# Pinning the TensorE instructions of the expert rounds to the order in which the kernel emits them

## The chip, the cores and the metric

The kernel runs on one core of one Trainium2 chip. The core has TensorE (PE in the profile, its weight loads PEld), VectorE (DVE), ScalarE (ACT), GpSimd (POOL) and the queue of SyncE (SP), which issues most of the transfers from HBM. The metric is the device time of one execution in microseconds (us), the median of several runs.

## The reference

Two blocks of two layers each work on 256 tokens of 1024 features in float32. Each of the four layers has a token mixer (RWKV-7, dilated attention, and twice a mixture of differential and sparse attention), and behind it a layer of 32 experts. The change lies in the expert layer alone. A router picks for each token one of four groups and two of its eight experts. The reference runs every expert over all tokens and multiplies by the gates, which are zero for experts that were not picked:

```python
hid = silu(einsum('td,edf->tef', xt, w_gate[gi])) * einsum('td,edf->tef', xt, w_up[gi])
hid = hid * gates[:, gi, :, None]
out = out + einsum('tef,efd->td', hid, w_down[gi])
```

The expert weights are the bulk of the input: per layer 32 experts with three matrices of 1024 x 256 numbers.

## The kernel before

The kernel is recorded through a tile layer whose scheduler decides the order of instructions on each engine. It ranks what is ready by a time model of its own, so TensorE's instructions may stand in another order than the Python code emits them. `keep_in_program_order` binds one instruction behind the one that was emitted before it on the same engine. It adds no wait for a semaphore, only a place in the queue.

An expert layer ("stage" below; there are four in a run, stage 1 to 4) gathers the tokens of each expert into 64 slots and works in 16 rounds, `g` = 0 to 15, two experts to a round. The rounds are written in `rounds_of`, and one round emits these parts for TensorE, in this order:

- `gate_up(g)` (line 331): 32 matmuls with 64 output rows, for the gate and the up matrix. The profile counts two records to each, since the operands are float32, so a round shows 64. ScalarE's Silu (line 334) and VectorE's product (line 336) make `hid` of the two results.
- `scatter(g - 1)` (line 366): 8 matmuls of 128 x 512 that add the last round's output rows `yh` and `yl` to the four accumulators `psc` (two token tiles by two halves of the features).
- `hid_t(g)` (line 342): two transposes of `hid`, which VectorE copies to `hT` (line 344).
- `scat(g + 1)` (lines 313 and 317): 6 small matmuls that make the scatter matrix and the gates of the next round.
- `gather`, two parts (line 300): 16 matmuls that collect the tokens of the next pair of rounds. In rounds 14 and 15 there is none.
- `down(g)` (line 353): 8 matmuls with 64 output rows, 16 records. VectorE (line 356, in stages 1 and 2 only) and the split of line 117 and 118 make `yh` and `yl` of them.

Matmuls with 64 output rows carry the form 128*64 in the profile, the others 128*128. Weights come in tiles of 1 MiB from 14 buffers, six tiles to a round, and round `g` asks for those of round `g + 3`; SyncE issues a load when the tile that held the buffer before has been read. Before round 0 stand `scat(0)` and all of `gather(0)`; behind round 15 comes the last `scatter`, and then a branch that skips further rounds when no expert has more than 64 tokens. They are skipped here: VectorE's line 336 ran 64 times in the whole execution, 16 rounds in each of four stages.

Of the kernel before, what the change touches and what calls it, by code (L numbers as in the profile page):

```python
# [26 lines left out]
P = 128  # L27
# [3 lines left out]
KD = 8  # L31
# [5 lines left out]
class Net:  # L37
# [17 lines left out]
    def wtile(self, name, own=False):  # L55
        """the next of the weight buffers, in turn with the extra ones where they are open"""
        pool, tag = self.wp, "w"
        if len(self.slots) > self.nw and not own:
            self.turn = (self.turn + 1) % len(self.slots)
            pool, tag = self.slots[self.turn]  # L60
        return pool.tile([P, 2048], F32, tag=tag, name=self.nm(name))
# [20 lines left out]
    def open_extra(self, n):  # L82
        """n more weight buffers, on the right side"""
        pool = self.extra.enter_context(self.tc.tile_pool(name=self.nm("extra"), bufs=n, side="right", reuse_waits="tile"))
        if len(self.slots) == self.nw:
            self.turn = -1
        self.slots += [(pool, "e")] * n
# [5 lines left out]
    def consts(self, scratch):  # L93
        nc = self.nc
        c = self.const
        jp = scratch        # [p, f] = f - p
# [5 lines left out]
        self.tri = c.tile([P, P], F32R, name="tri")         # [i, t] = 1 where t >= i  # L102
# [3 lines left out]
        self.iota64 = c.tile([P, CAP], F32, name="iota64")   # 1, ..., 64  # L106
# [8 lines left out]
    def split(self, hi, lo, src, eng=None):  # L115
        """hi + lo = src, each a float32r value."""
# [3 lines left out]
    def transpose_fm(self, dst, src):  # L120
        """dst[p, k, tok] = src[tok, tt, k, p]"""
# [17 lines left out]
class Moe:  # L139
    """w_g, w_u [32, 1024, 256]; w_d [32, 256, 1024]; scale [128, 512] x 2 multiplies the result"""  # L140
# [33 lines left out]
    def take(self, tt, xp, parts=False):  # L174
        """xp: the tokens of the tile tt [tok, k, p], feature 8p + k; parts: leaves their float32r parts in fs [p, k, t]"""
# [31 lines left out]
    def route(self):  # L207
# [16 lines left out]
        # the first of the largest  # L224
        v.tensor_tensor_scan(cu.rearrange("p t g -> p (t g)"), N.first4.rearrange("p t g -> p (t g)"),
                             t4.rearrange("p t g -> p (t g)"), 0.0, op0=OP.mult, op1=OP.add)
        # the two largest of each group, the first where they are equal
# [12 lines left out]
        # place of a token among those of its expert, from 1; 0 elsewhere  # L240
# [19 lines left out]
        # further rounds, for experts with more tokens than slots  # L260
# [18 lines left out]
    def rounds_of(self, load, acc, first, fills=None):  # L279
# [4 lines left out]
        w_g, w_u, w_d = self.w  # L284
        wt, xg, hid, hT, pt, gs, ys = {}, {}, {}, {}, {}, {}, {}
# [6 lines left out]
        def gather(b, k2):  # L292
# [3 lines left out]
            for kk in range(2):  # L296
                i = 0
                for tt in range(NT):
                    for xs in (xh, xl):
                        nc.tensor.matmul(ps[:, kk * 256:kk * 256 + 256], xs[:, tt, 2 * k2 + kk, :], pm[b][:, tt],  # L300
# [8 lines left out]
        def scat(g):  # L309
            b, o = g // 2, (g % 2) * P  # L310
            ps = N.psum("b")
            for tt in range(NT):
                nc.tensor.matmul(ps[:, tt * P:(tt + 1) * P], pm[b][:, tt, o:o + P], N.identr, start=True, stop=True)
            i = 0
            for tt in range(NT):
                for gp in (self.gh, self.gl):
                    nc.tensor.matmul(ps[:, 256:288], pm[b][:, tt, o:o + P], gp[:, tt], start=i == 0, stop=i == 3)  # L317
# [7 lines left out]
        def gate_up(g):  # L325
            b, o = g // 2, (g % 2) * P
            pg_, pu = N.psum("b"), N.psum("b")
            for nm, ps in (("g", pg_), ("u", pu)):
                for k in range(KD):
                    for c in range(2):  # L330
                        nc.tensor.matmul(ps[c * 64:c * 64 + 64, :256], xg[b][:, k, o + c * 64:o + c * 64 + 64],  # L331
# [7 lines left out]
        def hid_t(g):  # L339
            ps = N.psum("b")  # L340
            for j in range(2):
                nc.tensor.transpose(ps[:, j * P:(j + 1) * P], hid[g][:, j, :], N.ident)
# [3 lines left out]
        def down(g):  # L346
            yh = m2.tile([P, 2, 512], F32R, tag="yh", name=N.nm("yh"))
            yl = m2.tile([P, 2, 512], F32R, tag="yl", name=N.nm("yl"))
            for n in range(2):
                ps = N.psum("b")  # L350
                for j in range(2):
                    for c in range(2):
                        nc.tensor.matmul(ps[c * 64:c * 64 + 64, :], hT[g][:, j, c * 64:c * 64 + 64],  # L353
# [6 lines left out]
        def scatter(g):  # L360
# [4 lines left out]
            for i, tt, n in order:  # L365
                nc.tensor.matmul(acc[tt, n], pt[g][:, tt * P:(tt + 1) * P], ys[g][i][:, n], start=first and g == 0 and i == 0,
# [30 lines left out]
    def run(self, x, after_loads=None):  # L397
        """-> x + the sums of the experts, by token tile and half [128, 512], in PSUM"""
# [25 lines left out]
def rwkv_consts():  # L424
# [5 lines left out]
    for s in (16, 32):                                   # [t, i]: second block of two against the first  # L430
# [18 lines left out]
def wsplit(N, sp, w, eng=None, keep=False):  # L449
    """w [128, a, b] -> float32r parts, hi + lo = w; sp = pool, buffers of hi, of lo, and their tags"""  # L450
# [24 lines left out]
def weave(main, *fill, rest=True):  # L475
    """main's steps, with a step of the fillers (one after the other) behind each; then the rest of these"""
# [12 lines left out]
def every(gen, n):  # L489
    """a step of gen at each n-th of its own steps"""  # L490
# [9 lines left out]
def proj_fm_steps(N, sp, xh, xl, w, n0, evac, lay="(p k) n -> p k n"):  # L500
    """columns n0 .. n0+512 of x @ w, feature-major: evac(j, psum [128, 2 x 256]) for the tiles j, j + 1."""
# [3 lines left out]
    for k2 in range(KD // 2):  # L505
        wh, wl = wsplit(N, sp, parts[k2 // 2][:, 2 * (k2 % 2):2 * (k2 % 2) + 2])
        for lo in range(2):
            for j in range(4):
                o = pss[j // 2][:, (j % 2) * 256:(j % 2 + 1) * 256]
                ws = slice(j * P, (j + 1) * P)  # L510
                for kk in range(2):
# [4 lines left out]
                    else:  # L516
                        # the first product of a bank clears all of it
# [11 lines left out]
def proj_steps(N, sp, xh, xl, w, n0, evac, lay="(p k) n -> p k n", nk=KD):  # L529
    """columns n0 .. n0+512 of x @ w, token-major: evac(tt, psum [128, 512]).  The last step by token tile."""  # L530
# [22 lines left out]
def proj_tt(N, sp, xh, xl, w, n0, evac, lay="(p k) n -> p k n", subs="vggg", keep=True):  # L553
    """proj_steps by token tile, with all of the weights' parts on chip (sp may be one for each quarter): a step to split them,
    then one per token tile"""
# [15 lines left out]
def last_proj(N, sp, xh, xl, w, emit):  # L571
    """x @ w by halves, the second by token tile: emit(tt, n, psum [128, 512])"""
# [5 lines left out]
def split_tokens(N, xh, xl, tok, tt, eng=None):  # L578
    """tok(k): features k of the token tile tt [tok, 128] -> feature-major float32r parts"""
# [18 lines left out]
def rwkv(N, src, I, cst, emit, side, tail, scratch):  # L598
    """src: setup(tile) with tile() for [128, 8, 128], norm(tt), then tok(tt, k) gives [tok, p] (feature 8p + k); token
    mixing; emit(tt, n, psum [128, 512]).  Yields once before the last steps of the output projection."""  # L600
# [34 lines left out]
    pv = rp.tile([P, 7, KD], F32, name="pv")       # natural feature tiles: w0, a0 (by direction), k_k, k_a, r_k  # L635
# [20 lines left out]
    # ---- projections  # L656
# [16 lines left out]
    def shift(j, first=False):  # L673
        """the tokens mixed by mu[j], by halves of the features"""
# [72 lines left out]
    # ---- recurrence, in chunks of 64 tokens; the second direction runs on reversed tokens  # L747
# [5 lines left out]
    kn = p2.tile([P, KD, T], F32, name="kn")        # the removal key, normalised and negated  # L753
# [24 lines left out]
    def prep(z, e2, q2):  # L778
# [18 lines left out]
        E = q2.tile([P, 8, 65], F32, tag="E", name=N.nm("E"))           # 1, then the decay so far  # L797
# [81 lines left out]
    # inverses of the 16x16 diagonal blocks of I - N, a pair of chunks to a partition  # L879
# [40 lines left out]
    MQB = [p4.tile([P, 4, 4, P], F32, name=f"MQB{i}") for i in range(NB)]     # N, M, Q', B by pair  # L920
# [18 lines left out]
    def norm(z, e2):  # L939
        """group norm, bonus and output gate of 256 features: y in AR[z][e2][:, 0], (e, tt, 128) of each token"""  # L940
# [43 lines left out]
    def job(z, et, buf):  # L984
# [35 lines left out]
        # towards the chunk's end, and token-major  # L1020
# [52 lines left out]
        # inside the chunks  # L1073
# [7 lines left out]
        # [k, t] and [k', k] for the state's share; [v, t] and [v, k] of the chunk itself  # L1081
# [11 lines left out]
        RA = jp.tile([P, 2, 2, 2, 64], F32, tag="RA", name=N.nm("RA"), bufs=3)       # tile, (t | k), chunk  # L1093
# [49 lines left out]
    # ---- both directions, output projection  # L1143
# [45 lines left out]
def attn_consts():  # L1189
# [7 lines left out]
    a = np.stack(out, 1)                                        # [t, g, s]  # L1197
# [3 lines left out]
def dilated(N, src, I, cst, emit, tail=None):  # L1201
    """src: setup(tile) with tile() for [128, 1024], norm(tt), then tok(tt, k) gives [tok, p] (feature 8p + k);
    mixture of dilated attentions; emit(tt, n, psum [128, 512]).  Yields once before the output projection."""
# [114 lines left out]
def rope_setup(N, pos, c, scratch):  # L1318
    """cos | sin tables by token tile: cc [tok, tt, 2, 8] = cos, cos; ss = -sin, sin."""
# [32 lines left out]
def causal_setup(N, c):  # L1352
    """[t, 128 + s] = 0 where s <= t of a token tile, else -1e30; 0 before"""
# [8 lines left out]
def mixers(N, src, I, li, cs, caus, emit, tail=None):  # L1362
    """src: setup(tile), norm(tt), then tok(tt, k) gives [tok, p] (feature 128k + p); emit(tt, n, psum [128, 512]).
    Yields once before the output projection."""
# [15 lines left out]
    def fm_split(src, nk, tag, scale=1.0, ap=ap):  # L1380
        """src(tt, k) [128 tok, 128 features] -> feature-major float32r parts"""
# [660 lines left out]
```

## Time and profile before

| | |
|---|---|
| median of 3 runs | 2570.92 us (2564.14 to 2574.7) |
| span of the profiled execution | 2570.2 us |
| TensorE busy in it | 2341.1 us (91%) |
| mean granted clock of TensorE | 0.950 of full speed |

The span runs from the first to the last instruction of one execution. Its row is the nearest thing to that execution's own time that the profile has, and it stands 0.7 us below the median of the runs. A busy TensorE is not TensorE at its peak, since its matmuls overlap and their ends are modelled; where the text needs the length of something, it takes it from one start to another. Granted clock 1.00 is 2.4 GHz, the higher of the engine's two levels.

### The profile page before, as it was taken

Reading aid. Unit: us, or ns where it says so; the run is one execution under the profiler, and the core shown is the slowest. Engines: PE = TensorE matmul, PEld = TensorE weight load, DVE = VectorE, ACT = ScalarE, POOL = GpSimd, SP = SyncE. Lnnn points to the kernel's source line nnn. Section 1 sums busy time; section 2 is a strip of 40 time slices with the busy share of each in tenths; the row PEclk is TensorE's granted clock in tenths of the full one; section 3 lists DMA queues with packets and bytes.
Section 4 is the critical chain, followed back from the end, with each engine's and each line's share of the span. In section 5 each row is a group of like instructions: output and inputs, shape, how many; then the busy total and the mean of one; then the engine's idle time right before and its main releaser. Section 6 shows DMA issues by size and latency. Waiting matters only on the chain. (4 is left out here: it accounts for less than half of the span.)

```text
span 2570.2 us, 38418 instructions
## 1 busy us (share of the span) xinstructions
PE 2341.1 (91%) x15568; PEld 1682.7 (65%) x15568; DVE 1232.8 (48%) x2648; ACT 748.5 (29%) x1341; POOL 368.3 (14%) x292
## 2 busy tenths in 40 slices
PE   5976899988999799998999899989999799989997
PEld 2853577766665598986665477766665577766654
DVE  5678566764332435355332366573222576642222
ACT  2422243332111344442111235432111245421110
POOL 1243112230000221211000111220000222210000
PEclk7986899999999999998999889989999899989999
DMA  8425432258998362538999443477996443769993
GB/s 256 151 98 178 163 110 67 91 203 326 412 404 335 116 200 92 184 88 334 405 399 355 158 143 128 151 282 314 408 400 272 156 138 124 245 232 399 412 383 116
DMA packets 162988, 605.94 MB, mean 236 GB/s; under 512 B 36960, under 2 KB 37984, under 8 KB 107488
## 3 DMA queue, kind: packets, MB, share of 16 engines
q1 hardware_dynamic: 159072, 599.64, 62.4%
q0 software_dynamic: 3136, 3.16, 0.5%
q8 instruction: 131, 2.15, 0.3%
q10 hardware_dynamic: 576, 0.39, 0.1%
q14 instruction: 73, 0.60, 0.1%
HBM read 602.09 MB, written 1.05 MB: 235 GB/s over the span
## 5 line engine op out<-in xcount | busy, mean ns | idle before, releaser
L331 PE MATMUL psb<-w,xg 128*64 128x256 f32 x4096 | 474.3, 380 | 0.0
L331 PEld LDWEIGHTS psb<-w,xg 128*64 128x64 f32 x4096 | 297.8, 137 | 185.6 <-issue 48.1
L455 ACT ACTIVATE wh<-w 128x1024 fp32r<-128x1024 f32 x230 | 240.3, 1059 | 287.1 <-PE psb L545 147.7
L459 DVE TENSOR_TENSOR wl<-w,wh 128x1024 fp32r<-128x1024 f32 x150 | 202.6, 1357 | 167.8 <-ACT wh L455 142.5
L459 POOL TENSOR_TENSOR wl<-w,wh 128x1024 fp32r<-128x1024 f32 x80 | 198.3, 2481 | 576.6 <-ACT wh L455 466.4
L336 DVE SCALAR_TENSOR_TENSOR hid<-psb,gs,sg 128x256 f32<-128x256 f32 x64 | 43.0, 672 | 422.3 <-PE psb L331 422.3
L353 PE MATMUL psb<-w,hT 128*64 128x512 f32 x1024 | 234.1, 599 | 1.5 <-DVE hT L344 1.5
L544 PE MATMUL psb<-wh,xh 128*128 128x512 f32 x448 | 185.4, 415 | 5.6 <-ACT wh L455 2.4
L545 PE MATMUL psb<-wh,xl 128*128 128x512 f32 x448 | 181.3, 405 | 0.3 <-DVE xl L118 0.3
L118 DVE TENSOR_TENSOR yl<-psb,yh 128x512 fp32r<-128x512 f32 x128 | 88.4, 691 | 133.4 <-ACT yh L117 133.3
L117 ACT ACTIVATE yh<-psb 128x512 fp32r<-128x512 f32 x128 | 76.4, 597 | 255.9 <-DVE psb L356 140.7
L353 PEld LDWEIGHTS psb<-w,hT 128*64 128x64 f32 x1024 | 69.7, 136 | 118.3 <-issue 108.1
L542 PE MATMUL psb<-wl,xh 128*128 128x512 f32 x448 | 130.2, 398 | 3.3 <-POOL wl L459 1.7
L300 PE MATMUL psb<-pm,xh 128*128 128x256 f32 x512 | 130.7, 295 | 0.0
L321 ACT ACTIVATE pt<-psb 128x256 fp32r<-128x256 f32 x64 | 24.6, 384 | 347.9 <-PE psb L317 347.9
L300 PE MATMUL psb<-pm,xl 128*128 128x256 f32 x512 | 124.9, 283 | 0.0
L1742 PE MATMUL psb<-w,c_fm 128*32 128x512 f32 x384 | 85.6, 744 | 34.8 <-DMA w<-in_ada_w_dram 23.0
L544 PEld LDWEIGHTS psb<-wh,xh 128*128 128x128 f32 x448 | 86.5, 193 | 26.0 <-ACT wh L455 3.6
L542 PEld LDWEIGHTS psb<-wl,xh 128*128 128x128 f32 x448 | 84.9, 191 | 23.1 <-POOL wl L459 2.6
L545 PEld LDWEIGHTS psb<-wh,xl 128*128 128x128 f32 x448 | 86.9, 194 | 18.3 <-DVE xl L118 1.2
L300 PEld LDWEIGHTS psb<-pm,xl 128*128 128x128 f32 x512 | 98.7, 193 | 0.0
L300 PEld LDWEIGHTS psb<-pm,xh 128*128 128x128 f32 x512 | 98.6, 193 | 0.0
(540 smaller groups left out, 4167.3 us busy)
## 6 DMA issues: line engine op xcount, KB each, us to landing
w<-in_moe_w_gate_dram SPq DMA_DIRECT2D x64, 1024.0 KB, 7.8
w<-in_moe_w_up_dram SPq DMA_DIRECT2D x64, 1024.0 KB, 8.8
w<-in_moe_w_down_dram SPq DMA_DIRECT2D x64, 1024.0 KB, 10.0
w<-in_w_exp_gate_dram SPq DMA_DIRECT2D x64, 1024.0 KB, 7.9
w<-in_w_exp_up_dram SPq DMA_DIRECT2D x64, 1024.0 KB, 9.1
w<-in_w_exp_down_dram SPq DMA_DIRECT2D x64, 1024.0 KB, 10.4
w<-in_ada_w_dram SPq DMA_DIRECT2D x48, 1024.0 KB, 5.0
w<-in_w_in_dram SPq DMA_DIRECT2D x44, 1024.0 KB, 5.0
```

Of the source, the lines that this page charges most:

```text
L117: self.nc.scalar.activation(hi, src, AF.Copy)
L118: (eng or self.nc.vector).tensor_sub(lo, src, hi.bitcast(F32))
L300: nc.tensor.matmul(ps[:, kk * 256:kk * 256 + 256], xs[:, tt, 2 * k2 + kk, :], pm[b][:, tt], start=i == 0, stop=i == 3)
L331: nc.tensor.matmul(ps[c * 64:c * 64 + 64, :256], xg[b][:, k, o + c * 64:o + c * 64 + 64], wt[nm, 2 * g + c][:, k, :], start=k == 0, stop=k ...
L336: v.scalar_tensor_tensor(hid[g].rearrange("s j p -> s p j"), pu[:, :256].rearrange("s (p j) -> s p j", j=2), gs[g], sg.rearrange("s (p j) ...
L353: nc.tensor.matmul(ps[c * 64:c * 64 + 64, :], hT[g][:, j, c * 64:c * 64 + 64], wt["d", 2 * g + c][:, j, n * 512:(n + 1) * 512], start=j == ...
L455: nc.scalar.activation(wh, w, AF.Copy)
L459: i = (nc.gpsimd if eng == "g" else nc.vector).tensor_sub(wl, w, wh.bitcast(F32))
L542: nc.tensor.matmul(pss[tt], xh[:, k, t], wl[:, kk, :], start=False, stop=k == nk - 1)
L544: nc.tensor.matmul(pss[tt], xh[:, k, t], wh[:, kk, :], start=k == 0, stop=False)
L545: nc.tensor.matmul(pss[tt], xl[:, k, t], wh[:, kk, :], start=False, stop=False)
L1742: nc.tensor.matmul(ps[32 * j:32 * j + 32, :], self.c[:, k:k + 1].to_broadcast([P, 32]), wt[:, j * 512:(j + 1) * 512], start=k == 0, stop=k ...
```

## The change

Inside `rounds_of` every matmul goes through a helper `mm`, and each of the two transposes of `hid_t` likewise, and both call `keep_in_program_order`. Nothing else is altered but comments and docstrings. In the changed program the matmuls of these functions carry the line of the helper, 288, and lines below it are shifted by four.

```diff
+        keep = N.tc.keep_in_program_order
+
+        def mm(*a, **k):
+            keep(nc.tensor.matmul(*a, **k))
...
-                        nc.tensor.matmul(ps[:, kk * 256:kk * 256 + 256], xs[:, tt, 2 * k2 + kk, :], pm[b][:, tt],
+                        mm(ps[:, kk * 256:kk * 256 + 256], xs[:, tt, 2 * k2 + kk, :], pm[b][:, tt],
                                          start=i == 0, stop=i == 3)
...
-                nc.tensor.transpose(ps[:, j * P:(j + 1) * P], hid[g][:, j, :], N.ident)
+                keep(nc.tensor.transpose(ps[:, j * P:(j + 1) * P], hid[g][:, j, :], N.ident))
...
-                nc.tensor.matmul(acc[tt, n], pt[g][:, tt * P:(tt + 1) * P], ys[g][i][:, n], start=first and g == 0 and i == 0,
+                mm(acc[tt, n], pt[g][:, tt * P:(tt + 1) * P], ys[g][i][:, n], start=first and g == 0 and i == 0,
                                  stop=last and i == 1, skip_group_check=True)
```

What this moves on TensorE, outside the skipped further rounds, lies in three places. The first is round 10 of stage 1, where `psb_6402` and `psb_6403` are the gate and up results and `yh_6369`, `yl_6370` the output rows of round 9. Before, TensorE's queue read:

```order
L353 MATMUL psb_6379<-w_5937,hT_6335 64x512
L331 MATMUL psb_6402<-w_6044,xg_6235 64x256
L366 MATMUL psc_5148<-yh_6369,pt_6230 128x512
L366 MATMUL psc_5150<-yh_6369,pt_6230 128x512
L366 MATMUL psc_5148<-yl_6370,pt_6230 128x512
L366 MATMUL psc_5150<-yl_6370,pt_6230 128x512
L366 MATMUL psc_5149<-yh_6369,pt_6230 128x512
L366 MATMUL psc_5151<-yh_6369,pt_6230 128x512
L331 MATMUL psb_6402<-w_6046,xg_6235 64x256
```

and now, from the end of the same gate and up matmuls on, it reads:

```order
L288 MATMUL psb_6403<-w_6050,xg_6235 64x256
L288 MATMUL psc_5148<-yh_6369,pt_6230 128x512
L288 MATMUL psc_5149<-yh_6369,pt_6230 128x512
L288 MATMUL psc_5150<-yh_6369,pt_6230 128x512
L288 MATMUL psc_5151<-yh_6369,pt_6230 128x512
L288 MATMUL psc_5148<-yl_6370,pt_6230 128x512
L288 MATMUL psc_5149<-yl_6370,pt_6230 128x512
L288 MATMUL psc_5150<-yl_6370,pt_6230 128x512
L288 MATMUL psc_5151<-yl_6370,pt_6230 128x512
L346 MATMUL psb_6448<-ident,hid_6438 128x128 x2
```

The eight scatter matmuls had been put in between the gate and up matmuls; now they all stand behind them, ahead of the transposes of `hid`. This holds for rounds 9 to 15 of stages 1, 3 and 4 and rounds 8 to 15 of stage 2, 29 rounds. In stages 1 and 2 five or six of them had been split in three pieces as here (6 matmuls behind the first gate matmul, 2 behind the seventeenth), in stages 3 and 4 all eight stood behind the first gate matmul; the first split round of each stage had all eight behind the seventeenth, and round 15 began with two or five of them ahead of its first gate matmul. In some rounds 14 and 15 the eight matmuls of `down` had alternated between the two halves of the features; now the four of the first half come first. The rounds before the split ones are the same in both programs.

The second place is the start of stages 1 and 2, on TensorE behind the router's matmuls (`psb_5119`); `psb_5188` is `scat(0)`, `psb_5201` the first part of `gather(0)`. Before:

```order
L248 MATMUL psb_5119<-mask_5115,ones 128x32
L313 MATMUL psb_5188<-identr,pm_5130 128x128
L300 MATMUL psb_5201<-pm_5130,xh_4932 128x256
L313 MATMUL psb_5188<-identr,pm_5130 128x128
L300 MATMUL psb_5201<-pm_5130,xl_4933 128x256
L300 MATMUL psb_5201<-pm_5130,xh_4932 128x256
L300 MATMUL psb_5201<-pm_5130,xl_4933 128x256
L317 MATMUL psb_5188<-gh_5136,pm_5130 128x32
```

and now:

```order
L248 MATMUL psb_5119<-mask_5115,ones 128x32
L288 MATMUL psb_5188<-identr,pm_5130 128x128 x2
L288 MATMUL psb_5188<-gh_5136,pm_5130 128x32
L288 MATMUL psb_5188<-gl_5137,pm_5130 128x32
L288 MATMUL psb_5188<-gh_5136,pm_5130 128x32
L288 MATMUL psb_5188<-gl_5137,pm_5130 128x32
L288 MATMUL psb_5201<-pm_5130,xh_4932 128x256
```

Six gather matmuls that had stood among those of `scat(0)` now stand behind all of them. Stages 3 and 4 had this order already.

The third place is the last scatter of each stage, here on TensorE in stage 1, with `yh_6990` and `yl_6991` of round 15 and the four accumulators. Before:

```order
L366 MATMUL psc_5148<-yh_6990,pt_6893 128x512
L366 MATMUL psc_5150<-yh_6990,pt_6893 128x512
L366 MATMUL psc_5148<-yl_6991,pt_6893 128x512
L366 MATMUL psc_5150<-yl_6991,pt_6893 128x512
L366 MATMUL psc_5149<-yh_6990,pt_6893 128x512
L366 MATMUL psc_5151<-yh_6990,pt_6893 128x512
L366 MATMUL psc_5149<-yl_6991,pt_6893 128x512
L366 MATMUL psc_5151<-yl_6991,pt_6893 128x512
```

and now:

```order
L288 MATMUL psc_5148<-yh_6990,pt_6893 128x512
L288 MATMUL psc_5148<-yl_6991,pt_6893 128x512
L288 MATMUL psc_5149<-yh_6990,pt_6893 128x512
L288 MATMUL psc_5149<-yl_6991,pt_6893 128x512
L288 MATMUL psc_5150<-yh_6990,pt_6893 128x512
L288 MATMUL psc_5150<-yl_6991,pt_6893 128x512
L288 MATMUL psc_5151<-yh_6990,pt_6893 128x512
L288 MATMUL psc_5151<-yl_6991,pt_6893 128x512
```

The accumulators of the second half of the features (`psc_5149`, `psc_5151`) had come last; now the first token tile's two accumulators come first and those of the second tile last.

On the other engines little moves. In VectorE's queue the scaling of the second half (line 356) falls behind the split of the first half (line 118) in round 14 of stages 1 and 2 and round 15 of stage 2. In SyncE's queue one weight load of the following layer moves from behind the branch to ahead of it, after stages 1 and 3. ScalarE issues one small load one instruction later; GpSimd's order is the same.

## Rows read from the trace of the kernel before

**Rows 1.** The page's head: the span of the profiled execution.

```profile
span 2570.2 us, 38418 instructions
```

**Rows 2.** Waits of TensorE: engine, line, waited for, us in total, times, longest.

```profile
PE psb L342 <- DVE hid L336: 27.1, 33, 0.9
...
PE psc L366 <- ACT yh L117: 4.3, 15, 0.6
```

**Rows 3.** Timeline of TensorE, round 1 of stage 1: start, length, instruction, count.

```profile
617.00 7.08 PE L331 MATMUL psb<-w,xg 128*64 128x256 f32 x64
624.00 1.21 PE L366 MATMUL psc<-yh,pt 128*128 128x512 f32 x4
...
625.97 0.38 PE L342 MATMUL psb<-ident,hid 128*128 128x128 f32 x2
...
628.83 3.65 PE L353 MATMUL psb<-w,hT 128*64 128x512 f32 x16
...
632.31 7.08 PE L331 MATMUL psb<-w,xg 128*64 128x256 f32 x64
```

**Rows 4.** Timeline of TensorE, rounds 9 and 10 of stage 1.

```profile
739.50 4.05 PE L331 MATMUL psb<-w,xg 128*64 128x256 f32 x34
...
756.42 0.59 PE L331 MATMUL psb<-w,xg 128*64 128x256 f32 x2
...
758.32 0.73 PE L366 MATMUL psc<-yh,pt 128*128 128x512 f32 x2 [0.18 <-ACT yh L117]
...
762.59 0.73 PE L366 MATMUL psc<-yl,pt 128*128 128x512 f32 x2
...
767.75 0.44 PE L342 MATMUL psb<-ident,hid 128*128 128x128 f32 x2 [0.82 <-DVE hid L336]
...
774.14 0.59 PE L331 MATMUL psb<-w,xg 128*64 128x256 f32 x2
```

**Rows 5.** Timeline of TensorE, rounds 14 and 15 of stage 1.

```profile
838.61 0.44 PE L342 MATMUL psb<-ident,hid 128*128 128x128 f32 x2 [0.82 <-DVE hid L336]
...
839.62 3.68 PE L353 MATMUL psb<-w,hT 128*64 128x512 f32 x16
...
854.64 0.44 PE L342 MATMUL psb<-ident,hid 128*128 128x128 f32 x2 [0.81 <-DVE hid L336]
```

**Rows 6.** Timeline of TensorE, split rounds of stages 2 and 3.

```profile
1317.89 4.05 PE L331 MATMUL psb<-w,xg 128*64 128x256 f32 x34
...
1450.72 0.44 PE L342 MATMUL psb<-ident,hid 128*128 128x128 f32 x2 [0.81 <-DVE hid L336]
...
1888.49 4.05 PE L331 MATMUL psb<-w,xg 128*64 128x256 f32 x34
...
1905.38 0.59 PE L331 MATMUL psb<-w,xg 128*64 128x256 f32 x2
...
1999.01 0.43 PE L342 MATMUL psb<-ident,hid 128*128 128x128 f32 x2 [0.81 <-DVE hid L336]
```

**Rows 7.** Windows, round 8 of stage 1: length, engines' busy time, clock, DMA share, GB/s.

```profile
724.20:739.50 15.30, 15.30 (x114) 9.92 (x112) 5.45 (x12) 2.56 (x5) 0.00 (x0) 1.00 1.01 416
```

**Rows 8.** Timeline of SyncE's queue, first load of round 3's weights.

```profile
617.19 1.97 SPq L74 DMA_DIRECT2D w<-in_moe_w_gate_dram  x2
```

**Rows 9.** Transfers in round 8 of stage 1: count, size, us to landing.

```profile
w<-in_moe_w_down_dram SPq DMA_DIRECT2D x2, 1024.0 KB, 13.0
```

**Rows 10.** Timeline of TensorE, start of stage 1.

```profile
596.33 0.33 PE L313 MATMUL psb<-identr,pm 128*128 128x128 f32 x1 [0.81 <-DVE pm L275]
...
598.59 0.56 PE L300 MATMUL psb<-pm,xh 128*128 128x256 f32 x1
```

**Rows 11.** Timeline of VectorE, start of stage 1.

```profile
597.27 0.23 DVE L118 TENSOR_TENSOR gl<-gates,gh 128x64 fp32r<-128x64 f32 x1
```

**Rows 12.** Timeline of TensorE, end of stage 1.

```profile
862.96 0.73 PE L366 MATMUL psc<-yl,pt 128*128 128x512 f32 x2
```

**Rows 13.** Timeline of ScalarE, first instruction behind stage 1.

```profile
868.06 0.60 ACT L1773 ACTIVATE x<-psc 128x512 f32<-128x512 f32 x1 [5.88 <-PEq L404]
```

More of the change, by code (lines that the diff above doesn't have):

```diff
@@ L312, in scat @@
             for tt in range(NT):
-                nc.tensor.matmul(ps[:, tt * P:(tt + 1) * P], pm[b][:, tt, o:o + P], N.identr, start=True, stop=True)
+                mm(ps[:, tt * P:(tt + 1) * P], pm[b][:, tt, o:o + P], N.identr, start=True, stop=True)
             i = 0
@@ L316, in scat @@
                 for gp in (self.gh, self.gl):
-                    nc.tensor.matmul(ps[:, 256:288], pm[b][:, tt, o:o + P], gp[:, tt], start=i == 0, stop=i == 3)
+                    mm(ps[:, 256:288], pm[b][:, tt, o:o + P], gp[:, tt], start=i == 0, stop=i == 3)
                     i += 1
@@ L330, in gate_up @@
                     for c in range(2):
-                        nc.tensor.matmul(ps[c * 64:c * 64 + 64, :256], xg[b][:, k, o + c * 64:o + c * 64 + 64],
+                        mm(ps[c * 64:c * 64 + 64, :256], xg[b][:, k, o + c * 64:o + c * 64 + 64],
                                          wt[nm, 2 * g + c][:, k, :], start=k == 0, stop=k == KD - 1)
@@ L352, in down @@
                     for c in range(2):
-                        nc.tensor.matmul(ps[c * 64:c * 64 + 64, :], hT[g][:, j, c * 64:c * 64 + 64],
+                        mm(ps[c * 64:c * 64 + 64, :], hT[g][:, j, c * 64:c * 64 + 64],
                                          wt["d", 2 * g + c][:, j, n * 512:(n + 1) * 512], start=j == 0, stop=j == 1)
```

## The prediction

> **What bounds the kernel now.** I read the waits of TensorE first, then the timeline of one round in each order, then the windows and the transfers of the same stretch. In the expert stages TensorE has the work: in a round that already stands in emission order it is busy from end to end, at granted clock 1.00 (15.30 of 15.30 us, [rows 7]). No line of its waits names an expert weight. What it does wait for is in [rows 2]: 27.1 us in 33 waits of the `hid` transposes for VectorE's product, 4.3 us in 15 waits of the scatter for `yh`. 33 is the 29 split rounds and the four rounds 0, which have no scatter.
>
> The timeline shows why. A round in emission order runs gate and up, scatter, transposes, and the transposes start without a wait [rows 3]: while Silu and product are made, TensorE does the scatter. Round to round that is 632.31 - 617.00 = 15.31 us. In a split round the scatter has been done early, in between, and nothing is left to cover the product: the transposes wait 0.82 us [rows 4]. But the round is 774.14 - 756.42 = 17.72 us long, 2.41 us more for the same matmuls. So only a part of the loss is an idle time that the waits view names; the rest hides inside a busy TensorE. Of 2.41 us, 0.82 is that wait and 0.18 the scatter's wait for `yh` [rows 4]; 1.41 is left. A split round of stage 1 changes between the forms 128*64 and 128*128 four times more often than one in emission order (gate, scatter, gate, scatter, gate, transposes against gate, scatter with transposes). In stage 3 there are two more changes, and the round is 1905.38 - 1888.49 = 16.89 us long [rows 6]: 1.58 over 15.31, 0.77 without a like wait of 0.81. That is 0.35 us and 0.39 us to a change, one price from two shapes.
>
> The Trainium skill (TensorEngine Tiling, Key Properties) says that switching the tiling mode, other than going from one tile to another, drains TensorE. The two shapes of split rounds agree with it, at 0.35 and 0.39 us; without it the waits alone would be recovered, which is the first rival below.
>
> **The change part by part.** Stage 1, from the start of round 9 to the transposes of round 15: now 854.64 - 739.50 = 115.14 us [rows 4, 5]. In emission order it is five whole rounds, 5 x 15.31 = 76.55, then round 14 and 15, which have no gather: gate, up and scatter 625.97 - 617.00 = 8.97 [rows 3]; transposes to down 839.62 - 838.61 = 1.01 [rows 5]; down to the next gate 632.31 - 628.83 = 3.48 [rows 3]; gate, up and scatter of round 15 again 8.97. Sum 98.98, a gain of 16.16 us.
>
> Stage 2 splits from round 8: 1450.72 - 1317.89 = 132.83 us [rows 6] against 6 x 15.31 + 22.43 = 114.29, gain 18.54. Stage 3: 1999.01 - 1888.49 = 110.52 [rows 6] against 98.98, gain 11.54. Stage 4 repeats stage 3's pattern, 11.54 more. Together 57.8 us. I take it whole, since the emission order is no guess: these stages run eight or seven rounds in it already, with the same matmuls and buffers. The wait for `yh` goes with it, since the scatter then starts 7.0 us into the round (624.00 in [rows 3]).
>
> Start of stages 1 and 2: the six matmuls of `scat(0)` now come ahead of six gathers, and four of them need the split gates. `gl` is ready at 597.27 + 0.23 = 597.50 [rows 11]. Before, these twelve matmuls were issued in 598.59 - 596.33 = 2.26 us, 0.19 each, and the gathers filled the wait [rows 10]. Now the last `scat` matmul can't start before 597.50 + 2 x 0.19 = 597.9, and the six gathers follow it: done at about 599.2 against 598.59, 0.6 us late. Its bounds are 0 (the gates come no later than the queue) and 2.26 (the whole stretch is paid twice, as when a pause delays a rise of the clock). I take 1.0 in each of the two stages, nearer to the reckoning: 2.0 us.
>
> End of each stage: behind the last `yl` stand now five scatter matmuls, before it were two ([rows 12] is those two). Three more at (625.97 - 624.00) / 8 = 0.25 us [rows 3] are 0.74, in four stages 3.0 us. It counts, because ScalarE's first instruction behind the stage waits for TensorE's branch [rows 13]. Bounds: 0 (if the earlier finish of the first token tile gives it back) and 1.5 each, since VectorE's scaling of the second half now waits for the split of the first in stage 2.
>
> VectorE's swap in round 14 costs nothing, since the next scatter is a whole gate and up away; the load that moves ahead of the branch costs nothing as long as its buffer is free by the time TensorE reaches the branch, and the branch has until then. If it were not, every microsecond of it would count, once per stage in two stages; I keep 0 to 3 us for both.
>
> The pins themselves add no instruction and no semaphore. Sum: 57.8 - 2.0 - 3.0 = 52.8 us. The execution that was profiled has a span of 2570.2 [rows 1], so 2517.4; the median of the runs is 0.7 higher, which makes **2518 us**. Its own range is 2508 to 2528: start and end from 0 to their upper bounds, 0 to 10.5 us, the loads' 3 us, and the runs before, which stand 4 to 7 us from their median.
>
> **The rivals.**
>
> *Only the waits come back.* If the 1.4 and 0.8 us per round were work that any order pays, the gain would be 29 x 0.82 = 23.8 us, less the 5 of start and end: 2552 us. For it: the waits view names no more than that. Against it: the rounds of [rows 3] do the same matmuls without. Chance 0.06.
>
> *The weights become the bound.* A round uses 6 MiB, 6.29 MB. At 15.31 us that is 411 GB/s, and [rows 7] shows 416 with the transfer engines full (share 1.01), so a round could not go under 15.1 us by its transfers; the margin is 0.2 us. But the loads run ahead: round 3's are issued at 617.19 [rows 8] and used at 632.31 + 15.31 = 647.62, a lead of 30.4 us, and late in the eight fast rounds they take 13.0 us to land [rows 9]. That leaves 17.4 us, and round 12 issues the last. If transfers gave only 6.29 / 17.72 us = 355 GB/s, as in split rounds, a round would fall behind by 2.41 us, 28.9 in twelve rounds, 11.5 beyond the slack: 46 us in four stages, and 2564 in all. Against it: seven fast rounds lie behind the one of [rows 7], and it still moved 416. Chance 0.04.
>
> The Trainium skill (HBM Reference, Specifications) gives each core of a pair about 358 GB/s, and more to one that streams alone; by the lower figure this rival's 2564 would be the time, while the 416 of [rows 7] goes with the higher.
>
> *Something other than the order made the late rounds long.* Then they stay at 17.72 and 16.89, and the time is 2571 to 2576 us. Against it: stage 2 is split one round earlier than the others, and it is one round earlier that it slows. Chance 0.03.
>
> *The rests were what kept the clock up: slower than before.* A split round rests for 0.8 us, one in emission order not at all. If the granted clock fell from 1.00 to the lower level under 240 us of unbroken work, a round would cost up to 15.3 us more; from four such rounds (52.8 / 15.3 = 3.5) the change loses, and seven of them in one stage make it 2518 + 107 = 2625 us. Against it: eight rounds without a rest ran at 1.00, the last of them [rows 7]. Chance 0.03.
>
> **How the numbers follow.** The forecast has 0.81; 0.03 is for a greater gain, with the following layers' loads meeting emptier queues, down to 2500. The range that should hold 8 in 10 is 2507 to 2533: the forecast's own, with a little of the first rival's side. A measurement of this kernel can tell about 0.5%, 13 us, from no change. Faster by more than that: 0.81 + 0.03 + 0.06 + a part of the transfers' rival, 0.91; within it 0.06; slower 0.03.
>
> **What would show it.** In the profile after, all rounds 1 to 13 of a stage should be 15.3 us apart, gate and up should stand as one block of 64 records, and the wait for `hid` should be left in four rounds 0 only, some 3.4 us. The scatter should wait for `yh` at the end of the stages alone. The transfers should be full until round 12's loads have landed, with landing times of up to 15 us; times that grow round by round, or a wait of line 288 for a weight, would be the second rival, a granted clock under 1.00 inside a stage the fourth. If the blocks are whole and the rounds still take 16 us or more, the price of the changes of form was wrong.

## The result, and the profile after

The changed kernel takes 2514.84 us (median of 4 runs, 2505.15 to 2515.97) against 2571.61 for the kernel before beside it: ratio 0.9773, 95% interval 0.9748 to 0.9797. The forecast was 2518 us, with a range of 2507 to 2533. The profiled span fell by 2570.2 - 2514.1 = 56.1 us:

```profile
span 2514.1 us, 38422 instructions
```

That is four instructions more than before. The page counts the same number for TensorE, VectorE, ScalarE and GpSimd in both kernels, so the four are among those that it does not count as busy (register, branch, semaphore and DMA-issuing ones).

TensorE's waits in the expert rounds (engine, line, waited for, us in total, times, longest), to be held against [rows 2]; line 346 was 342 before, and 288 now stands for every matmul of the rounds:

```profile
PE psb L346 <- DVE hid L340: 3.4, 4, 0.9
...
PE psc L288 <- ACT yh L117: 1.5, 2, 0.7
...
PE psc L288 <- DVE yl L118: 0.9, 4, 0.2
```

The 33 waits of the transposes have become the four of the rounds 0, and the scatter waits at the stage ends alone. Round 9 of stage 1 and the start of round 10, which [rows 4] showed torn apart (start, length, instruction, count):

```profile
737.98 7.08 PE L288 MATMUL psb<-w,xg 128*64 128x256 f32 x64
744.98 1.21 PE L288 MATMUL psc<-yh,pt 128*128 128x512 f32 x4
746.03 1.09 PE L288 MATMUL psc<-yl,pt 128*128 128x512 f32 x4
746.95 0.38 PE L346 MATMUL psb<-ident,hid 128*128 128x128 f32 x2
...
749.81 3.65 PE L288 MATMUL psb<-w,hT 128*64 128x512 f32 x16
753.29 7.08 PE L288 MATMUL psb<-w,xg 128*64 128x256 f32 x64
```

Gate and up are one block of 64 records, the transposes wait for nothing, and the round takes 753.29 - 737.98 = 15.31 us. All rounds 1 to 13 of the four stages lie within 15.29 to 15.32. Windows of rounds 9, 10 and 12 of stage 1 and of one of stage 3, the later lines beside [rows 7] (length, busy time of the five engines, granted clock, share of the transfer engines, GB/s):

```profile
737.97:753.28 15.31, 15.31 (x114) 9.94 (x112) 4.81 (x10) 2.56 (x5) 0.00 (x0) 1.00 1.01 414
753.28:768.60 15.32, 15.32 (x114) 9.94 (x112) 5.49 (x12) 2.56 (x5) 0.00 (x0) 1.00 1.00 404
...
784.00:799.20 15.20, 15.20 (x114) 9.86 (x112) 4.70 (x10) 2.56 (x5) 0.00 (x0) 1.00 1.01 416
1800.37:1815.67 15.30, 15.30 (x114) 9.93 (x113) 3.50 (x7) 2.56 (x5) 0.00 (x0) 1.00 1.01 416
```

The clock stays at 1.00 and the transfers are full, as they were in round 8 before. Landing in round 12 of stage 1 (count, size, us to landing) is no longer than in [rows 9], and line 288 has no wait for a weight:

```profile
w<-in_moe_w_down_dram SPq DMA_DIRECT2D x2, 1024.0 KB, 13.1
```

Where the 56.1 us came from, each read between the same two instructions of the two traces:

| stretch | before | after | gain |
|---|---|---|---|
| transposes of round 0 to those of round 15, four stages | 244.04, 246.41, 239.35, 239.33 | 227.85, 227.85, 227.67, 227.67 | 58.1 |
| first `scat` matmul to first gate matmul, stages 1, 2 | 6.29, 6.77 | 8.29, 8.38 | -3.6 |
| transposes of round 15 to the end of the last scatter | 9.05, 7.75, 6.83, 6.84 | 10.19, 8.44, 7.44, 7.41 | -3.0 |
| all the rest, where no order changed | | | 4.6 |

The last line is of the other layers: the way to stage 1 was 3.5 us shorter, between stages 1 and 2 it was 3.5 shorter, between 3 and 4 it was 2.9 longer, and what stands behind stage 4 was 1.0 shorter. In the profiles of the experiments below, whose kernels are the same up to there, the first `scat` matmul of stage 1 comes anywhere from 588.8 to 598.2 us, so I count this line as the spread between executions and not as the change's.

### The profile page after: what moved, and what is told of

It reads as the page before. It is cut to its first block, busy times and chain, and to the rows that moved or that the text cites. A ratio compares the mean times of both kernels' runs of the same rounds, so it can differ in the third digit from the quotient of the medians.

```text
span 2514.1 us, 38422 instructions
## 1 busy us (share of the span) xinstructions
PE 2311.8 (92%) x15568; PEld 1686.2 (67%) x15568; DVE 1234.3 (49%) x2648; ACT 748.5 (30%) x1341; POOL 368.1 (15%) x292
## 5 line engine op out<-in xcount | busy, mean ns | idle before, releaser
L288 PE MATMUL psb<-w,xg 128*64 128x256 f32 x4096 | 453.2, 379 | 0.0
```

Source lines behind the costliest of these rows:

```text
L288: keep(nc.tensor.matmul(*a, **k))
```

## Experiments

The forecast split the 2.41 us of a torn round into waits (0.82 and 0.18) and four changes of form at 0.35 each. **Theory A** is that price. Two changes, from 128*64 to 128*128 and back, are called a return trip below. **Rival B**: only visible waits cost. **Rival C**: any break in the run of gate and up matmuls costs, whatever the form of what stands in it. Each run below is the changed kernel with the edit shown, in all 60 rounds 1 to 15 unless the text says otherwise; `scatter(g, lo, hi)` does matmuls lo to hi of the eight.

**Two changes of form.**

```diff
 # gate_up(g), behind the 16 gate matmuls
+                if g > 0 and nm == "g":
+                    scatter(g - 1, 0, 2)
 # the round
-                scatter(g - 1)
+                scatter(g - 1, 2, 8)
```

> Two of the eight scatter matmuls stand between the gate and the up matmuls in rounds 1 to 15 of all four stages, the other six behind up as in the changed kernel. That is two more changes between the forms 128*64 and 128*128 in a round, with no new wait: six matmuls, 6 x 0.25 = 1.5 us, still cover the 0.82 us that the product needs. Theory A (each change of form costs 0.35 to 0.39 us): rounds of 16.0 to 16.1 us, 60 of them at 0.70 to 0.78 more, 42 to 47 us on 2515: 2557 to 2562 us. Rival B (only the visible waits cost): rounds of 15.31 and 2515. Rival C (any break in the run of gate and up matmuls costs, whatever the form of what stands in it): as A.

Measured 2539.68 us (2534.14 to 2545.74). One round of stage 1 in its timeline:

```profile
722.14 3.62 PE L288 MATMUL psb<-w,xg 128*64 128x256 f32 x32
725.70 0.73 PE L288 MATMUL psc<-yh,pt 128*128 128x512 f32 x2
726.35 3.67 PE L288 MATMUL psb<-w,xg 128*64 128x256 f32 x32
729.96 0.73 PE L288 MATMUL psc<-yh,pt 128*128 128x512 f32 x2
...
737.80 0.39 PE L288 MATMUL psb<-w,xg 128*64 128x256 f32 x2
```

There is no wait, and the round is 737.80 - 722.14 = 15.66 us: 0.35 more for two changes, half of what A asked (15.69 in stages 3 and 4, 0.38 more). B is out, and A's price is twice too high.

**Four changes of form**: one scatter matmul behind each half of the gate matmuls.

```diff
+                    if g > 0 and nm == "g" and k in (3, 7):
+                        scatter(g - 1, k // 4, k // 4 + 1)
```

> One scatter matmul stands behind the first half of the gate matmuls and one behind the second half, the other six behind up: four more changes of form in a round than in the changed kernel, and no new wait. Theory A: 1.40 to 1.56 us more in each of 60 rounds, rounds of 16.7 to 16.9, 2599 to 2609 us. Rival B: rounds of 15.31 and 2515. Rival C: two breaks instead of one, so twice what the run with two changes shows, as A.

Measured 2553.83 us (2550.83 to 2563.54), a missed expectation again: rounds of 16.01 us, 0.70 more, twice the run above. So a return trip costs 0.35 us (0.38 in stages 3 and 4 of the run above), 0.17 to a change.

**The wait alone.**

```diff
-            if g > 0:
-                scatter(g - 1)
             hid_t(g)
+            if g > 0:
+                scatter(g - 1)
```

> The whole scatter stands behind the transposes instead of ahead of them: no more changes of form than in the changed kernel, but nothing covers VectorE's product. Theories A, B and C agree that the wait of the transposes for hid (0.82 to 0.85 us) comes back in 60 rounds: rounds of 16.13, 49 us, 2564 us, and nothing hidden beside it. If a round took 16.9 or more, the hidden part of the split rounds would come with the wait and not with the changes of form, against A.

Measured 2569.34 us (2560.32 to 2572.82), with this row among the waits:

```profile
PE psb L346 <- DVE hid L340: 54.5, 64, 0.9
```

Rounds take 16.19 to 16.21 us (16.14 to 16.18 in stage 3): the wait's 0.86 (0.84) and 0.02 to 0.03 beside it, some 0.88 and 0.87 together. What was hidden in the split rounds does not come with the wait.

**The same place, the same form**: half of `down` between gate and up.

```diff
+                if g > 0 and nm == "g":
+                    down(g - 1, (1,))
...
-            down(g)
+            down(g, (0, 1) if g == NGRP - 1 else (0,))
```

> Half of the down matmuls of the round before (four matmuls, eight records, form 128*64) stand between the gate and the up matmuls; the scatter is whole behind up. The run of gate and up is broken in the same place as with two scatter matmuls there, by more work, but the form does not change. No work is added. Theory A: rounds of 15.3 us, 2515 us. Rival C: 0.7 us more in each of 60 rounds, about 2557 us. What could blur it: the second half's output rows come 3.5 us later, but the scatter starts 8.8 us into the round, so no wait is expected.

Measured 2517.92 us (2515.89 to 2521.37). Two starts of gate, a round apart:

```profile
723.26 3.62 PE L288 MATMUL psb<-w,xg 128*64 128x256 f32 x32
726.71 1.89 PE L288 MATMUL psb<-w,hT 128*64 128x512 f32 x8
728.43 3.62 PE L288 MATMUL psb<-w,xg 128*64 128x256 f32 x32
...
738.57 0.60 PE L288 MATMUL psb<-w,xg 128*64 128x256 f32 x4
```

15.31 us. C is out: a break costs only where the form changes.

These four leave a hole. In stage 3 a split round lost 1.59 us, of which the wait is 0.87 and the return trip 0.38; in stage 1 it lost 2.41, of which 0.88 and 0.70. Some 0.34 and 0.83 are unpaid. [Rows 4] shows what my runs did not copy: before its first break a split round has x2, the two records of one matmul. A step of gate is a pair of matmuls, with 64 columns of the engine (the 64 output rows) for the left expert and 64 for the right. Looked at closely, inside a whole block two records start at once, every 0.21 us (timeline of the changed kernel, cut to a few tenths of a microsecond):

```profile
615.90 0.39 PE L288 MATMUL psb<-w,xg 128*64 128x256 f32 x2
...
616.12 0.39 PE L288 MATMUL psb<-w,xg 128*64 128x256 f32 x2
```

and in the kernel before, ahead of the break, only one:

```profile
756.42 0.38 PE L331 MATMUL psb<-w,xg 128*64 128x256 f32 x1
756.63 0.38 PE L331 MATMUL psb<-w,xg 128*64 128x256 f32 x1
```

The lone matmul takes the time of a pair. I took it that its partner behind the break does so again, at every break. **Theory D**: return trip 0.35 us, and some 0.4 us for a torn pair.

**A torn pair, first try**: two scatter matmuls behind the first gate matmul.

```diff
+                        if g > 0 and nm == "g" and (k, c) == (0, 0):
+                            scatter(g - 1, 0, 2)
```

> Like the run with two changes, but the two scatter matmuls stand behind the first gate matmul alone, between the two experts' matmuls of one step (the 64 columns of the left and of the right expert), as in the kernel before, and not behind the last pair. Theory D, formed on the first four runs: a return trip between the forms costs 0.345 us (15.655 - 15.31, and half of 16.005 - 15.31), and a pair of 64-column matmuls that is torn apart loses its overlap; the split rounds of before leave (17.72 - 15.31 - 0.82 - 0.18 - 2 x 0.345) / 2 = 0.36 us for one torn pair, (16.89 - 15.31 - 0.82 - 0.345) = 0.41 in stages 3 and 4. D expects rounds of 15.655 + 0.36 to 0.43 = 16.0 to 16.1 us, 2556 to 2562 us. Rival (the rest of the split rounds' loss lies elsewhere, as in the wait or in the number of scatter matmuls in between): rounds of 15.66 as with two changes, 2535 to 2540 us.

Measured 2603.73 us (2596.48 to 2605.11), outside what any theory gave. Stage 1 of its timeline says why:

```profile
724.69 0.49 PE L288 MATMUL psc<-yh,pt 128*128 128x512 f32 x1
726.07 0.50 PE L288 MATMUL psc<-yh,pt 128*128 128x512 f32 x1 [0.88 <-ACT yh L117]
726.50 7.12 PE L288 MATMUL psb<-w,xg 128*64 128x256 f32 x62
```

The second scatter matmul stands too early for its `yh`. I had overlooked that: the first six scatter matmuls of a split round in stage 1 began with the half that is ready. Stages 3 and 4, without VectorE's scaling, show no wait there and 16.21 us a round, but the two runs' difference could hold a wait too short to be named, so it was done again.

**A torn pair, without the wait**: the same behind the left expert's last gate matmul, `(k, c) == (KD - 1, 0)`.

> Two scatter matmuls stand inside the last pair of gate matmuls (between the left and the right expert's), the other six behind up: one return trip between the forms, one torn pair, and the scatter late enough that its data are there, which the earlier run with a torn pair lacked. Theory D, torn pair with a change of form: 15.655 + 0.37 to 0.39 = 16.03 to 16.05 us a round in all four stages, against 15.655 to 15.685 for the same two matmuls behind the whole pair; 60 rounds, 22 to 24 us above that run's span of 2532.4, so about 2555 to 2560 us. Rival (the earlier run's loss was its waits alone): 15.66 to 15.69 a round and 2532 to 2540 us.

Measured 2561.88 us (2559.79 to 2565.89):

```profile
728.41 3.62 PE L288 MATMUL psb<-w,xg 128*64 128x256 f32 x30
731.96 0.73 PE L288 MATMUL psc<-yh,pt 128*128 128x512 f32 x2
732.62 4.10 PE L288 MATMUL psb<-w,xg 128*64 128x256 f32 x34
```

30 and 34 records instead of 32 and 32, one matmul moved over the break, and rounds of 16.07 us in all stages. Against the run with two changes that is 16.07 - 15.66 = 0.41 in stages 1 and 2, 0.38 in stages 3 and 4, for the torn pair.

**A torn pair without a change of form**: the run with half of `down` in between, with the place `(k, c) == (0, 0)`.

> Half of the down matmuls of the round before stand between the two experts' first gate matmuls: a torn pair without a change of form. Theory D: rounds of 15.31 + 0.36 to 0.43 = 15.7 us, 60 rounds, 2515 + 22 to 26 = 2537 to 2543 us. If a torn pair costs nothing without a change of form, since a neighbour of the same form can overlap with either half: rounds of 15.31, 2515 to 2518 us.

Measured 2518.04 us (2515.15 to 2521.08): rounds of 15.36 us, so 0.05 for the tear, and D as I had put it is wrong here. The timeline shows the other expectation:

```profile
725.31 0.38 PE L288 MATMUL psb<-w,xg 128*64 128x256 f32 x1
725.32 0.64 PE L288 MATMUL psb<-w,hT 128*64 128x512 f32 x1
```

The lone gate matmul starts beside one of `down`. Here a matmul of 64 columns finds a partner in a neighbour of its form, whichever part that belongs to, and every lone one in the traces shown stands right ahead of a change of form. The Trainium skill (TensorEngine Tiling, Key Properties) says that different tiles work independently and that a change of the mode drains the engine. The rows agree with that; the page has no price, and here a tear costs 0.05 us without a change of form and 0.41 us with one.

The same holds inside the split rounds of the kernel before, and it corrects the count. Round 10 of stage 1, cut to a few tenths of a microsecond at each place:

```profile
756.94 0.73 PE L366 MATMUL psc<-yh,pt 128*128 128x512 f32 x2
...
758.99 0.44 PE L331 MATMUL psb<-w,xg 128*64 128x256 f32 x2
...
762.28 0.39 PE L331 MATMUL psb<-w,xg 128*64 128x256 f32 x2
...
766.33 0.38 PE L331 MATMUL psb<-w,xg 128*64 128x256 f32 x1
766.54 0.38 PE L331 MATMUL psb<-w,xg 128*64 128x256 f32 x1
```

Right behind the first break two records start at once: the right expert's matmul runs beside the left one of the next step. The 16 matmuls between the two breaks (758.99 to 762.59, [rows 4]) run in pairs to the end. Only the first gate matmul (756.42 above) and the last up matmul (766.33) are alone. Two lone matmuls in place of one pair are the time of one pair more, so this round lost one tear of 0.41 us and not two.

What is left of its 0.83 us is the scatter's wait for `yh`, which costs more than the 0.18 of its row. Its six scatter matmuls take 758.99 - 756.94 = 2.05 us; in stage 3 all eight, without a wait, take 1907.96 - 1905.91 = 2.05:

```profile
1905.91 1.20 PE L366 MATMUL psc<-yh,pt 128*128 128x512 f32 x4
...
1907.96 7.12 PE L331 MATMUL psb<-w,xg 128*64 128x256 f32 x62
```

A scatter matmul more takes 0.23 us ((746.95 - 746.03) / 4 in the changed kernel), so the wait costs about 0.46, which is 0.28 more than the row names. The first try with a torn pair shows the same surplus: its two scatter matmuls take 726.50 - 724.69 = 1.81 us against 732.62 - 731.96 = 0.66 without a wait, 1.15 for a wait that is named with 0.88.

**All eight between gate and up**, behind whole pairs.

```diff
+                if g > 0 and nm == "g":
+                    scatter(g - 1, 0, 8)
```

> All eight scatter matmuls stand between the last gate and the first up matmul in rounds 1 to 15: two changes of form, no torn pair, and nothing that covers the product. Theory D: 15.31 + 0.345 + 0.86 = 16.5 us a round, 2514 + 60 x 1.2 = 2586 us. The prediction's price of a change (0.35 to 0.39 us each): 15.31 + 0.70 to 0.78 + 0.86 = 16.9 us, 2608 to 2614 us, as the split rounds of stages 3 and 4 before.

Measured 2590.15 us (2585.37 to 2594.99), rounds of 16.54 us (16.53 in stages 3 and 4). That is return trip and wait as D adds them (16.5), not the 16.9 of the prediction's price. It also shows that the return trip costs this much when the scatter stays in one piece. It is the split round of stage 3 with its pair left whole, and 16.90 - 16.53 = 0.37 is the tear.

**The order mended by hand.** Round 0 does its transposes between the two gather parts, round 14's last four scatter matmuls stand behind the transposes of round 15, `scat(0)`'s gate matmuls behind the first part of `gather(0)`, and the last scatter does the first half of the features first. The edit without the lines that split `scat` in two for it:

```diff
+            order.sort(key=lambda a: (a[2], a[0], a[1]))    # last scatter
...
+                scatter(g - 1, 0, 4 if g == NGRP - 1 else 8)
+                hid_t(g)
+            if g == NGRP - 1:
+                scatter(g - 1, 4, 8)
...
                 gather(b + 1, 2 * q)
+                if g == 0:
+                    hid_t(0)
                 gather(b + 1, 2 * q + 1)
```

> The changed kernel with its emission order mended where waits were left: round 0 gives its transposes after scat(1) and half of the gather (0.85 us of wait in each of four stages), the last four matmuls of the scatter of round 14 stand behind the transposes of round 15 (0.52 us of wait for hT in three stages), the gate matmuls of scat(0) stand behind the first quarter of gather(0) (0.7 to 0.9 us in two stages), and the last scatter does the first half of the features before the second (0.6 to 1.1 us in four stages). Expected sum: 3.4 + 1.5 + 1.6 + 2.8 = 9 us, 2506 us, with the rounds themselves at 15.31. Rival: the transfers are full in these rounds, or the clock's rise at the start of stages 1 and 2 sets when they begin, and no more than 3 to 5 us come: 2510 to 2513.

Measured 2511.12 us (2508.33 to 2513.64), ratio to before 0.9769, interval 0.9750 to 0.9789. From the first gate matmul to the end of the last scatter the stages take 243.99, 242.12, 240.95 and 240.91 us against 246.02, 244.27, 243.10 and 243.07: 8.5 less. The starts of stages 1 and 2 take 6.40 and 7.85 us, 2.4 less together. Yet the span is only 4.8 less: the other layers were 6.0 longer, 2.8 of it ahead of stage 1, where the two kernels are the same, and 0.8 behind stage 4, where the tail is 15.51 us against 14.74.

**The start of before, pinned.** The same without the new order of the last scatter, and with `scat(0)` and `gather(0)` interleaved in the order of the kernel before, beside a second set of the changed kernel.

> The order mended by hand, but the start of each stage interleaved exactly as in the kernel before, and the last scatter in the emission order of the changed kernel. Start of stages 1 and 2, from the first scat matmul to the first gate matmul: 6.3 to 6.8 us if the order sets it, 7.7 to 8.5 as in the pinned runs if the clock at that point does. From the first gate matmul to the end of the last scatter 244.6, 242.8, 241.6, 241.6 us in the four stages (changed kernel less 0.85 for round 0 and 0.5 for round 15, the latter in three stages). Sum in the median: 2 to 4 us below the changed kernel that runs beside it if the other layers stay as long, and what is below 5 us can't be told from none by the median.

> The changed kernel again, beside the two others: 2510 to 2518 us, rounds of 15.31 us, 7.7 to 8.5 us from the first scat matmul to the first gate matmul in stages 1 and 2.

Measured 2512.43 us (2506.81 to 2514.88, ratio 0.9774, interval 0.9760 to 0.9789), and the changed kernel 2518.67 (2512.23 to 2525.90, ratio 0.9811, 0.9797 to 0.9824). The stages are shorter, as worked out to within 0.5: 244.66, 243.31, 241.64, 241.65 us. The median does not settle which is faster: within this set the mended order leads by 0.25%, but the changed kernel itself gave 0.9773 in its first set and 0.9811 in this one, and the spans of the two profiled runs are 2510.7 and 2510.4. The start tells more (timeline of the run with the start of before):

```profile
593.36 0.33 PE L288 MATMUL psb<-identr,pm 128*128 128x128 f32 x1 [0.80 <-DVE pm L275]
...
601.35 0.44 PE L288 MATMUL psb<-w,xg 128*64 128x256 f32 x2
```

In the order of before it takes 601.35 - 593.36 = 7.99 us (7.92 in stage 2), nearly as long as pinned (8.26 and 8.45 beside it), not 6.29. The order alone does not set it; most of it is the clock. In windows of the start of stage 1 the last number but two is the granted clock. In the changed kernel:

```profile
592.81:600.10 7.29, 7.13 (x31) 6.90 (x32) 2.62 (x14) 1.24 (x3) 0.00 (x0) 0.50 0.01 3
600.18:601.10 0.92, 0.92 (x9) 0.79 (x8) 0.00 (x0) 0.88 (x2) 0.00 (x0) 1.00 0.00 0
```

in the run with the start of before:

```profile
594.32:601.10 6.78, 6.78 (x32) 6.78 (x32) 1.66 (x8) 2.22 (x4) 0.00 (x0) 0.50 0.01 2
```

and in the kernel before:

```profile
596.66:596.83 0.17, 0.17 (x2) 0.17 (x2) 0.17 (x4) 0.00 (x0) 0.00 (x0) 1.00 0.00 0
...
597.01:600.20 3.19, 3.19 (x16) 3.19 (x16) 1.24 (x7) 1.21 (x3) 0.00 (x0) 0.50 0.02 5
...
600.42:602.50 2.08, 2.08 (x20) 2.06 (x18) 0.69 (x1) 0.69 (x2) 0.00 (x0) 1.00 0.00 0
```

With the same order the lower level lasted some 3.4 us there and 6.8 us in the run.

## Why the prediction was right, point by point

- *Late rounds at 15.31 us in all stages, 57.8 us.* Measured 58.1. The emission order is no guess where half of the stage already runs in it.
- *What a split round lost.* Its parts were wrong although their sum was right. The step that failed is "1.41 is left ... That is 0.35 us and 0.39 us to a change, one price from two shapes". A change costs 0.17. In stage 3 as much again was the torn pair; in stage 1 the 1.41 was two return trips (0.70), one torn pair (0.41) and 0.28 of the scatter's wait beyond the 0.18 that its row names. The sums now close to 0.04 us: stage 1, 15.31 + 0.88 (wait of the transposes) + 0.70 + 0.41 + 0.46 (wait of the scatter) = 17.76 against 17.72; round 9 of stage 1, which has one break and no wait of the scatter, 15.31 + 0.88 + 0.35 + 0.41 = 16.95 against 756.42 - 739.50 = 16.92 [rows 4]; stage 3, 15.30 + 0.87 + 0.38 + 0.38 = 16.93 against 16.90. That the two shapes of [rows 4] and [rows 6] gave nearly the same quotient was chance, since different things stood in them. The forecast did not hang on it, since the emission order has none of them.
- *Start of stages 1 and 2, 2.0 us.* 3.6, inside the bounds of 0 to 2.26 each, but most of it by the clock and not by the wait for `gl`: with the order of before it is 0.3 and 0.5 shorter, no more. Why the one profile of before had the clock back some 3 us earlier in both stages is open; with one profile of before, this part may be a difference between executions and not the change's.
- *End, 3.0 us.* 3.0 to the end of the last scatter (1.14, 0.69, 0.61, 0.57). What follows it was not always later by as much: ScalarE's first work behind the stage is 2.0 later in stage 1, 0.1 in stage 2.
- *The median 0.7 above the span, and 2518.* The median is 3 us lower; the measured values of the three terms give 51.5, and the other layers' 4.6 made it 56.1. By its own terms the forecast of 52.8 was 1.3 off.
- *Rivals.* Only the waits: refused, rounds would be 16.9 and 16.1 us. Transfers as the bound: 404 to 416 GB/s at full share and no wait for a weight. Something other than the order: refused by the runs that put breaks back into every round, with early rounds as long as late ones. A falling clock: 1.00 in every window of a stage after its start.
- *The pins add no instruction and no semaphore.* The page counts four instructions more, none among those that it counts by engine; what they are is open.

## What to carry to other kernels

A wait that the profile names can be the smaller half of what an order costs, and can itself cost more than its row says (0.46 us for a row of 0.18 here): measure from start to start of the same block in both orders, and take the difference apart. Where matmuls fill only half of the columns, keep them in pairs and their pairs in one run; what is put in between is cheap if it has the same form (0 to 0.05 us here) and dear if it has not (0.35 us, about 0.75 where it also leaves an odd matmul on either side). Two shapes that agree on a price do not show what is priced; an edit that separates the parts does.

## What the runs showed of the hardware that was not expected

- A matmul of 64 columns alone takes as long as two that stand together: one record or two start every 0.21 us.
- At the start of stages 1 and 2, behind or soon after waits of 2.2 and 0.8 us for VectorE, the granted clock falls to 0.50 (the level of 1.2 GHz; gathers start every 0.21 us) and comes back to 1.00 (every 0.12 us). In stage 1 of the kernel before it was still 1.00 at the first `scat` matmul; in that of the changed kernel it was 0.50 there. It came back 4.1 and 4.6 us behind the first `scat` matmul in the kernel before, 6.1 to 7.8 us in all 20 starts of the ten profiles with the emission order there, 7.7 in both with the order of before, and 4.4 and 6.9 with the one mended by hand.
- The rounds are now nearly balanced: 15.31 us of TensorE, and 6.29 MB at 416 GB/s, 15.1 us, of transfers.
